# Three experts in plain fp32, two products side by side in the array, woven buffer by buffer with the five others

## The chip, the core and the metric

The kernel runs on one core of a Trainium2 chip. The time is device microseconds for one execution of the whole program. The kernel before takes 2594.24 us (median of 3 runs, 2590.64 to 2599.49).

## What is computed

Two decoder blocks of two layers each, one after the other, on 256 tokens of width 1024, in fp32. The change touches only the last part, the mixture of experts (MoE) that ends the second block: eight experts of hidden width 3584, and each token goes to two of them.

```python
def moe_swiglu(h, router, w_gate, w_up, w_down):
    bsz, seq, d = h.shape
    t = h.reshape(-1, d)
    logits = (t @ router).astype(jnp.float32)
    top_v, top_i = lax.top_k(logits, TOP_K)
    top_w = jax.nn.softmax(top_v, axis=-1)
    gates = jnp.sum(jax.nn.one_hot(top_i, N_EXPERTS, dtype=jnp.float32) * top_w[..., None], axis=1)
    out = jnp.zeros(t.shape, jnp.float32)
    for e in range(N_EXPERTS):
        y_e = swiglu(t, w_gate[e], w_up[e], w_down[e]).astype(jnp.float32)
        out = out + gates[:, e:e + 1] * y_e
    return out.astype(h.dtype).reshape(bsz, seq, d)
```

`swiglu(h, ...)` is `(silu(h @ w_gate) * (h @ w_up)) @ w_down`. The weights of the eight experts are 352 MB, of the 560 MB that the kernel reads.

## The kernel before

Products keep fp32 accuracy by splitting. Each operand x becomes H, x rounded to the format fp32r that TensorE takes in one pass, and L = x - H, also fp32r; `mm3` (line 226) then adds three products, H*H, H*L and L*H. `weights` (line 207) does this for weights: SyncE (SP) issues a load of 128 x 2048 numbers (1 MB) into a buffer of the ring `raw`, ScalarE (ACT) casts it into a buffer of the ring `wh` (line 222), VectorE (DVE) subtracts into one of the ring `wl` (line 223). The rings are lists of pools that are taken in turn; in the MoE there are 5 buffers of raw and 3 each of wh and wl. A raw buffer is free when the subtraction is done, wh and wl when TensorE (PE) is done with them.

The MoE begins by ranking the experts by how many tokens they got (`moe_order`, line 2068). The five fullest have 128 places (here: wide), the other three 64 (tight; `PLACES`, line 1980). `moe_gather` (line 2170) brings the tokens of a group of experts (`TOGETHER`, line 1982) into place with a one-hot product and splits them; `moe_places` makes the transposed one-hot for the way back. `moe_pass` (line 2241) then goes through the experts in order. An expert is four steps of 1024, 1024, 1024 and 512 hidden columns. For each step `half` does the gate product (four buffers of weights, two in the last step) and then the up product (as many); `gate` applies silu and `hidden` multiplies; `turn` transposes the result on PE and splits it; `down` multiplies by w_down (four buffers, two in the last step), adding up over the expert in two PSUM banks, `py`. That is 42 buffers an expert. In the program's order the gate and up products of step i+1 stand before the down product of step i. After an expert's last step `combine` splits the result, brings it back to the tokens with the transposed one-hot (lines 2347 and 2348), and adds it into the output, weighted by the gate (line 2349).

A tight expert uses the 64 free places otherwise: H and L of its tokens stand side by side in the 128 stationary columns, so two products a piece are enough (line 2263), with wh and with wl. They leave two partial results in partitions 0 to 63 and 64 to 127, which `whole` (line 2281) adds up.

PSUM has eight banks: four in pool "a" (`half`) and four in pool "b" (`turn`, `py`, `combine`, `moe_gather`, `moe_places`). A planner puts the instructions of each engine in order, by their place in the program and by when it reckons their inputs and buffers to be ready; on the chip each engine goes through its own list in that order. Line 751, in an earlier part of the kernel, is a plain fp32 product with 64 stationary columns; two heads in turn write to partitions 0 to 63 and 64 to 127 of the same bank, with line 752 behind each. After the MoE a branch handles tokens beyond an expert's places; here it isn't taken.

Of the kernel before, what the change touches and what calls it, by code (L numbers as in the profile page):

```python
# [11 lines left out]
F32 = mybir.dt.float32  # L12
# [42 lines left out]
class Core:  # L55
# [65 lines left out]
    @contextmanager  # L121
    def phase(s, raw, split, work):

        with ExitStack() as c:
            pool = lambda nm, n: c.enter_context(s.tc.tile_pool(name=f"{nm}{s.uid()}", bufs=n, reuse_waits="tile"))
            s.ring = {nm: [pool(nm, n)] * n for nm, n in (("raw", raw), ("wh", split), ("wl", split))}
            s.t2p = pool("t2", work)
            yield

    @contextmanager  # L130
    def wider(s, **more):

        with ExitStack() as c:
# [3 lines left out]
            s.turn = 0  # L137
            yield

    turn = 0  # L140
# [66 lines left out]
    def weights(s, src, k0, nk, c0, cn, rows="k p"):  # L207
# [5 lines left out]
        raw, H, L = (s.ring[nm][s.turn % len(s.ring[nm])].tile([128, 2048], dt, tag=nm, name=f"{nm}{s.n}")  # L213
                     for nm, dt in (("raw", F32), ("wh", F32R), ("wl", F32R)))
        s.turn += 1
# [8 lines left out]
        return v(H), v(L)  # L224

# [1750 lines left out]
class MoE:  # L1976
# [125 lines left out]
    def moe(s, N):  # L2102
# [6 lines left out]
        s.moe_pass(N, N.slot, s.PLACES, s.TOGETHER, first, ahead)  # L2109
# [3 lines left out]
        with s.tc.If(n > 0):  # L2113
            rest = s.small([128, 2, s.E], "slotb")
            nc.vector.tensor_sub(rest, N.slot, bc(s.caps, 2))
            s.moe_pass(N, rest, s.REST, s.TOGETHER_REST, s.moe_gather(N, rest, s.TOGETHER_REST[0], s.REST))
            s.moe_store()
# [52 lines left out]
    def moe_gather(s, N, slot, js, places):  # L2170
# [20 lines left out]
        for d in range(0, ND, 2):  # L2191
            p = s.psum("b")
            for m in range(2):
                for h, src in enumerate((N.H, N.L)):
                    for t in range(2):
                        nc.tensor.matmul(p[:, m * W:m * W + W], src[d // 2][:, t, m * 128:m * 128 + 128], P[:, t, :W],
                                         start=(h == 0 and t == 0 and m == 0), stop=(h == 1 and t == 1),
                                         skip_group_check=True)
            for m in range(2):
                x = s.t2([128, 512], "xe", F32R)  # L2200
                x = x[:, :2 * W].rearrange("p (a j c) -> p j a c" if wide else "p (j a c) -> p j a c", a=2, j=len(js))
                v, g = p[:, m * W:m * W + W].rearrange("p (j c) -> p j c", j=len(js)), s.col("ln_ffn_2", 8 + d + m)
                nc.scalar.activation(x[:, :, 0], v, AF.Copy, scale=g)
                nc.vector.scalar_tensor_tensor(x[:, :, 1], v, g, f(x[:, :, 0]), op0=OP.mult, op1=OP.subtract)
                X.append(x)
        return {j: [X, i, places[j], P] for i, j in enumerate(js)}

    def moe_places(s, N, G):
# [3 lines left out]
        p = s.psum("b")  # L2212
        n = next(iter(G.values()))[2]
        for X, i, n, P in G.values():
            for t in range(2):
                nc.tensor.matmul(p[:n, i:i + 1], f(P[:, t, i * n:i * n + n]), N.rc[:, t:t + 1], start=(i == 0 and t == 0),
                                 stop=(t == 1), skip_group_check=True)
        nc.vector.tensor_copy(rc[:n], p[:n, :len(G)])
        for g in G.values():
            X, i, n, P = g  # L2220
            PT = s.t2([128, 2, 128], "onehotT", F32R)
            x = P[:, :, i * n:i * n + n]
            if n == 64:
                y = s.t2([128, 512], "eyH", F32R)[:, :256].rearrange("p (t c) -> p t c", t=2)
                for u in range(2):
                    nc.vector.tensor_copy(y[:, :, u * 64:u * 64 + 64], f(x))
                x = y
            p = s.psum("b", dt=F32R)
            for t in range(2):
                nc.tensor.transpose(p[:, t * 128:t * 128 + 128], x[:, t], s.identR)  # L2230
            nc.scalar.copy(PT, p[:, :256].rearrange("p (t c) -> p t c", t=2))
            g += [PT, rc[:n, i:i + 1]]

    AHEAD = 3
    WIDE = 1024

# [4 lines left out]
    def moe_pass(s, N, slot, places, together, G, ahead=()):  # L2241
# [3 lines left out]
        steps = [(j, f0, min(s.WIDE, s.FE - f0)) for j in range(s.E) for f0 in range(0, s.FE, s.WIDE)]  # L2245
        per = len(steps) // s.E
        py = {}
        ahead = list(ahead)
        most = places is s.PLACES
# [7 lines left out]
        def product(o, j, x, w, start, stop):  # L2257


            if x.shape[2] == 64:  # L2260
                x = x.rearrange("p a c -> p (a c)")
                for h in range(2):
                    nc.tensor.matmul(o, x, w[h], start=start and h == 0, stop=stop and h == 1, skip_group_check=True)  # L2263
            else:
                s.mm3(o, (x[:, 0], x[:, 1]), w, start, stop)

        def half(i, nm):

            j, f0, fn = steps[i]
            X, u = G[j][:2]  # L2270
            p = [s.psum("a") for _ in range(fn // 512)]
            nk = 2048 // fn
            for k0 in range(0, ND, nk):
                w = ahead.pop(0) if ahead else weights(nm, j, 128 * k0, nk, f0, fn)
                for k in range(nk):
                    for c, o in enumerate(p):
                        product(o, j, X[k0 + k][:, u], [x[:, k, c * 512:c * 512 + 512] for x in w],
                                k0 + k == 0, k0 + k == ND - 1)
            return p

        def whole(p, n):

            if n == 128:
                return p
            a = s.t2([64, 512], "eb")
            nc.scalar.copy(a, p[64:])
            nc.vector.tensor_add(a, p[:64], a)
            return a

        def gate(i, pg):  # L2290
            n, rc = G[steps[i][0]][2], G[steps[i][0]][5]
            out = []
            for p in pg:
                out.append(s.t2([n, 512], "eh"))
                nc.scalar.activation(out[-1], whole(p, n), AF.Silu, scale=rc)
# [133 lines left out]
```

## Time and profile before

| | |
|---|---|
| median of 3 runs | 2594.24 us |
| the profiled execution | 2596.73 us, span 2595.0 us |
| granted TensorE clock, mean | 0.968 |
| PE busy over the span | 2423.1 us |
| VectorE busy | 2004.4 us |
| ScalarE busy | 1550.8 us |
| loaded from memory | 555.88 MB |

All rows come from one profiled execution; times in them are microseconds from its span's start unless marked ns. Busy time of an engine is the time in which it executes an instruction; matmuls overlap each other, so their pitch, the time from the start of one to the start of the next, tells more than their length. A wait is put down to the instruction that released it last.

### The profile page before, as it was taken

The numbers are of one execution on the slowest core, as the hardware profiler recorded it, in microseconds if no ns is written. First come the engines' busy times: TensorE is split into PE (matmuls) and PEld (weight loads), VectorE is DVE, ScalarE is ACT, GpSimd is POOL, SyncE is SP. The second block draws the span as 40 slices with busy tenths as digits, with TensorE's granted clock in tenths as the row PEclk, the third lists the DMA queues.
The fourth block names the chain that finished last, engine by engine and source line by source line (L and its number), as shares of the span: only waits on it lengthen the run. The fifth ranks groups of instructions, "written<-read, shape, count | busy, mean of one in ns | idle before, by whom it ended". The sixth has DMA issues, their size and how long they took to land.

```text
span 2595.0 us, 39887 instructions
## 1 busy us (share of the span) xinstructions
PE 2423.1 (93%) x15462; PEld 2122.8 (82%) x15462; DVE 2004.4 (77%) x3186; ACT 1550.8 (60%) x2313; POOL 88.0 (3%) x180
## 2 busy tenths in 40 slices
PE   7988799999998999899999999999999999988887
PEld 6867689999888999789999888888888877655654
DVE  6876477658886765766658876888888888999998
ACT  4553355445555544564455645776777777878776
POOL 2011010000001000000000000000000000000000
PEclk9998699999999999989999998999999999999999
DMA  5312345555434555425554213999999998999997
GB/s 166 111 58 34 62 166 167 178 178 162 131 109 137 165 178 183 146 82 184 183 172 130 87 45 131 343 359 349 368 329 365 346 360 325 371 379 363 372 369 281
DMA packets 266195, 559.59 MB, mean 216 GB/s; under 512 B 12751, under 2 KB 172510, under 8 KB 251662
## 3 DMA queue, kind: packets, MB, share of 16 engines
q1 hardware_dynamic: 264544, 555.71, 61.2%
q0 software_dynamic: 1328, 1.22, 0.9%
q8 instruction: 123, 2.02, 0.3%
q14 instruction: 74, 0.61, 0.1%
q10 hardware_dynamic: 126, 0.03, 0.0%
HBM read 555.88 MB, written 1.05 MB: 215 GB/s over the span
## 4 chain that ended last, share of the span: by engine, by line
PE 69%; DVE 15%; issue 6%; ACT 4%; POOL 2%; DMA 2%; DVEq 0%; ACTq 0%; POOLq 0%; SPq 0%
PE pa L230 16%; PE pa L231 16%; PE pa L229 16%; DVE wl L223 9%; ACT wh L222 2%; PE pb L230 2%; PE pb L231 2%; PE pb L229 2%; PE pb L1167 2%; PE pb L1792 2%; PE pa L2263 1%; PE pb L1481 1%; PE pb L2263 1%; PE pb L1133 1%; DMA ssmvb<-in_ssm_a_log_dram 1%
## 5 line engine op out<-in xcount | busy, mean ns | idle before, releaser
L223 DVE TENSOR_TENSOR wl<-raw,wh 128x512 fp32r<-128x512 f32 (+1 forms) x1108 | 1258.7, 1166 | 212.3 <-ACT wh L222 207.1
L222 ACT CAST wh<-raw 128x512 fp32r<-128x512 f32 (+1 forms) x1108 | 1063.6, 1004 | 559.3 <-issue 266.3
L229 PE MATMUL pa<-xH,wh 128*128 128x256 f32 (+1 forms) x1936 | 553.2, 286 | 16.0 <-ACT xH L313 8.1
L230 PE MATMUL pa<-xL,wh 128*128 128x256 f32 (+1 forms) x1936 | 553.3, 286 | 0.5 <-DVE xL L314 0.5
L231 PE MATMUL pa<-xH,wl 128*128 128x256 f32 (+1 forms) x1936 | 552.8, 286 | 1.0 <-DVE wl L223 1.0
L229 PEld LDWEIGHTS pa<-xH,wh 128*128 128x128 f32 (+1 forms) x1936 | 372.3, 193 | 18.1 <-ACT xH L313 8.8
L230 PEld LDWEIGHTS pa<-xL,wh 128*128 128x128 f32 (+1 forms) x1936 | 372.3, 192 | 3.5 <-DVE xL L314 2.0
L231 PEld LDWEIGHTS pa<-xH,wl 128*128 128x128 f32 (+1 forms) x1936 | 372.2, 192 | 2.9 <-DVE wl L223 1.9
L230 PE MATMUL pa<-wl,xe 128*128 128x512 f32 x560 | 221.1, 395 | 7.7 <-DVE wl L223 7.7
L231 PE MATMUL pa<-wh,xe 128*128 128x512 f32 x560 | 219.7, 392 | 0.0
L229 PE MATMUL pa<-wh,xe 128*128 128x512 f32 x560 | 207.7, 393 | 0.0
L2263 PE MATMUL pa<-wl,xe 128*128 128x512 f32 x336 | 131.2, 424 | 36.8 <-DVE wl L223 34.0
L229 PE MATMUL pa<-hidH,wh 128*128 128x256 f32 x528 | 149.4, 283 | 0.0
L230 PE MATMUL pa<-hidL,wh 128*128 128x256 f32 x528 | 149.4, 283 | 0.0
L231 PE MATMUL pa<-hidH,wl 128*128 128x256 f32 x528 | 149.4, 283 | 0.0
L230 PEld LDWEIGHTS pa<-wl,xe 128*128 128x128 f32 x560 | 105.7, 189 | 34.0 <-DVE wl L223 12.8
L2263 PE MATMUL pa<-wh,xe 128*128 128x512 f32 x336 | 123.7, 402 | 3.5 <-ACT wh L222 3.5
L229 PEld LDWEIGHTS pa<-wh,xe 128*128 128x128 f32 x560 | 105.6, 189 | 21.3
L231 PEld LDWEIGHTS pa<-wh,xe 128*128 128x128 f32 x560 | 105.6, 189 | 21.0
L2263 PEld LDWEIGHTS pa<-wl,xe 128*128 128x128 f32 x336 | 59.6, 192 | 76.3 <-DVE wl L223 67.0
L230 PE MATMUL pb<-wl,ehH 128*128 128x512 f32 x280 | 111.2, 397 | 0.9 <-DVE wl L223 0.9
L231 PE MATMUL pb<-wh,ehL 128*128 128x512 f32 x280 | 109.4, 391 | 0.0
(813 smaller groups left out, 4078.8 us busy)
## 6 DMA issues: line engine op xcount, KB each, us to landing
raw<-in_o_moe_w_gate_dram SPq DMA_DIRECT2D x112, 1024.0 KB
raw<-in_o_moe_w_up_dram SPq DMA_DIRECT2D x112, 1024.0 KB
raw<-in_o_moe_w_down_dram SPq DMA_DIRECT2D x112, 1024.0 KB
raw<-in_ffn_w_dram SPq DMA_DIRECT2D x60, 1024.0 KB
raw<-in_od_w_in_dram SPq DMA_DIRECT2D x20, 1024.0 KB
raw<-in_o_w_in_dram SPq DMA_DIRECT2D x16, 1024.0 KB
raw<-in_e_ffn_w_gate_dram SPq DMA_DIRECT2D x11, 1024.0 KB
raw<-in_e_ffn_w_up_dram SPq DMA_DIRECT2D x11, 1024.0 KB
```

Of the source, the lines that this page charges most:

```text
L222: nc.scalar.copy(H[:, c:e], raw[:, c:e])
L223: nc.vector.tensor_sub(L[:, c:e], raw[:, c:e], f(H[:, c:e]))
L229: mm(out, a[0], b[0], start=start, stop=False, skip_group_check=True)
L230: mm(out, a[0], b[1], start=False, stop=False, skip_group_check=True)
L231: mm(out, a[1], b[0], start=False, stop=stop, skip_group_check=True)
L1133: nc.tensor.matmul(p[:, k * 128:k * 128 + 128], NT[:, k, :], X[:, k, :], start=True, stop=True)
L1167: mm = lambda o, a, b, st=True, sp=True: nc.tensor.matmul(o, a, b, start=st, stop=sp, skip_group_check=True)
L1481: mm = lambda o, a, b, st, sp: nc.tensor.matmul(o, a, b, start=st, stop=sp, skip_group_check=True)
L1792: mm = lambda o, a, b, st=True, sp=True: nc.tensor.matmul(o, a, b, start=st, stop=sp, skip_group_check=True)
L2263: nc.tensor.matmul(o, x, w[h], start=start and h == 0, stop=stop and h == 1, skip_group_check=True)
```

## The change

The tight experts' weights are no longer split. They are loaded into a raw buffer (`whole_weights`) and multiplied as they are, in plain fp32, by 64 stationary columns of tokens that aren't split either. Each pair of products, for the two halves of the columns, writes to partitions 0 to 63 and 64 to 127 of one bank, so that they can stand side by side in the array. Their hidden values lie on 128 partitions with half as many columns, are transposed as 128 x 128 blocks and not split; their result is in one bank rather than two, and goes back to the tokens in plain fp32 with 64 rows.

The three tight experts also no longer come after the five wide ones. `moe_pass` is now two lanes (`moe_lane`), generators that yield after each buffer of weights: the wide lane starts with eight buffers (`LEAD`), then one buffer of the tight lane is put behind each 1.6 buffers of the wide one, so that both end together. All of the tight lane's PSUM banks but its result come from pool "a" (`side`); the wide lane keeps to its pools. The rings now have a turn of their own each, as raw is used without wh and wl. The tight gather stands behind the first eight buffers.

```diff
+    def buffer(s, nm):
+        i = s.turns[nm]
+        s.turns[nm] += 1
+        return s.ring[nm][i % len(s.ring[nm])].tile([128, 2048], F32 if nm == "raw" else F32R, tag=nm,
+                                                    name=f"{nm}{s.n}")
...
+    def whole_weights(s, src, k0, nk, c0, cn, rows="k p"):
+        s.n += 1
+        v = s.buffer("raw")[:, :nk * cn].rearrange("p (k c) -> p k c", k=nk)
+        s.nc.sync.dma_start(v, src[k0:k0 + 128 * nk, c0:c0 + cn].rearrange(f"({rows}) c -> p k c", p=128))
+        return v
...
+    LEAD = 8
...
-    def moe_pass(s, N, slot, places, together, G, ahead=()):
+    def moe_pass(s, N, first, ahead):
+        wide = [x for x in s.TOGETHER if s.PLACES[x[0]] == 128]
+        tight = [x for x in s.TOGETHER if s.PLACES[x[0]] == 64]
+        a = s.moe_lane(N, N.slot, s.PLACES, wide, first, ahead, True)
+        per = 3 * D * s.FE // (128 * 2048)
+        na, nb = per * sum(map(len, wide)), per * sum(map(len, tight))
+        for _ in range(s.LEAD):
+            next(a)
+        na -= s.LEAD
+        b = s.moe_lane(N, N.slot, s.PLACES, tight, s.moe_gather(N, N.slot, tight[0], s.PLACES, "a"), side="a")
+        due = 0
+        for _ in range(na):
+            next(a, None)
+            due += nb
+            while due >= na:
+                due -= na
+                next(b, None)
+        for x in (a, b):
+            for _ in x:
+                pass
...
-            return s.weights(w[e] if isinstance(e, int) else w[bass.ds(e, 1)].rearrange("o r c -> (o r) c"), *a)
+            w = w[e] if isinstance(e, int) else w[bass.ds(e, 1)].rearrange("o r c -> (o r) c")
+            return s.weights(w, *a) if places[j] == 128 else s.whole_weights(w, *a)
...
         def half(i, nm):
...
-            p = [s.psum("a") for _ in range(fn // 512)]
+            p = [s.psum("a") for _ in range(fn // 512 if wide else 1)]
             nk = 2048 // fn
+            hw = fn // 2
             for k0 in range(0, ND, nk):
                 w = ahead.pop(0) if ahead else weights(nm, j, 128 * k0, nk, f0, fn)
                 for k in range(nk):
...
+                    if wide:
+                        x = X[k0 + k][:, u]
+                        for c, o in enumerate(p):
+                            s.mm3(o, (x[:, 0], x[:, 1]), [x[:, k, c * 512:c * 512 + 512] for x in w], start, stop)
+                    else:
+                        for c in range(2):
+                            mm(p[0][64 * c:64 * c + 64, :hw], X[k0 + k][:, u], w[:, k, c * hw:c * hw + hw],
+                               start=start, stop=stop, skip_group_check=True)
+                yield
...
         def turn(i, h):
...
-                p = s.psum("b")
+                p = s.psum(side)
...
+                if wide:
+                    H, L = s.t2([128, n, 128], "ehH", F32R), s.t2([128, n, 128], "ehL", F32R)
+                    s.split(v, H, L)
+                    out.append((H, L))
                 else:
+                    y = s.t2([128, n, 128], "ehT")
+                    nc.scalar.copy(y, v)
+                    out.append(y)
...
         def down(i, hs):
...
-                py[j] = [s.psum("b"), s.psum("b")]
+                py[j] = [s.psum("b") for _ in range(2 if wide else 1)]
...
+                    else:
+                        a, q = divmod(k0 + k, fn // 256)
+                        for c in range(2):
+                            mm(py[j][0][64 * c:64 * c + 64], hs[0][:, q, 64 * a:64 * a + 64],
+                               w[:, k, c * 512:c * 512 + 512], start=start, stop=stop, skip_group_check=True)
+                yield
...
         def combine(j):
...
+                    p = s.psum(side)
+                    if wide:
+                        mm(p, PT[:, t, :], yH, start=True, stop=False)
+                        mm(p, PT[:, t, :], yL, start=False, stop=True)
+                    else:
+                        mm(p, f(PT[64 * c:64 * c + 64, t, :]), y[64 * c:64 * c + 64], start=True, stop=True)
```

## Rows read from the trace of the kernel before

**Rows 1.** The page, engines: busy us, share of the span, instructions.
```profile
PE 2423.1 (93%) x15462; PEld 2122.8 (82%) x15462; DVE 2004.4 (77%) x3186; ACT 1550.8 (60%) x2313; POOL 88.0 (3%) x180
```
**Rows 2.** Stretch: its us, busy PE PEld DVE ACT POOL, clock, DMA share, GB/s.
```profile
1620.00:2215.00 595.00, 585.47 (x2687) 481.83 (x2686) 518.50 (x329) 427.57 (x304) 0.00 (x0) 1.00 0.95 351
2240.00:2570.00 330.00, 276.58 (x1045) 190.34 (x1046) 314.92 (x217) 258.54 (x203) 0.00 (x0) 0.96 0.98 373
```
**Rows 3.** Timeline: start, length, what; first wide and tight products, combines.
```profile
1601.63 0.77 PE L229 MATMUL pa<-wh,xe 128*128 128x512 f32 x1
...
2225.76 0.39 PE L2263 MATMUL pa<-wh,xe 128*128 128x512 f32 x1
...
2253.64 0.63 PE L2347 MATMUL pb<-eyH,onehotT 128*128 128x512 f32 x2
...
2490.48 0.62 PE L2347 MATMUL pb<-eyH,onehotT 128*128 128x512 f32 x2
...
2584.14 0.74 PE L2347 MATMUL pb<-eyH,onehotT 128*128 128x512 f32 x2 [0.21 <-ACT eyH L288]
```
**Rows 4.** Timeline of PE: two fp32r products of 512 columns in a wide expert.
```profile
1700.02 0.39 PE L230 MATMUL pa<-wl,xe 128*128 128x512 f32 x1
1700.24 0.39 PE L231 MATMUL pa<-wh,xe 128*128 128x512 f32 x1
```
**Rows 5.** Groups from 1560 us on: count | busy us, mean ns | idle before.
```profile
L223 DVE TENSOR_TENSOR wl<-raw,wh 128x2048 fp32r<-128x2048 f32 x333 | 752.4, 2286 | 74.0 <-ACT wh L222 72.1
L222 ACT CAST wh<-raw 128x2048 fp32r<-128x2048 f32 x333 | 631.9, 1911 | 127.3 <-PE pa L231 62.2 <-PE pb L231 34.7 <-PE pb L2263 8.8
...
L291 DVE TENSOR_TENSOR ehL<-pb,ehH 128x512 fp32r<-128x512 f32 x35 | 24.0, 685 | 3.3 <-ACT ehH L288 3.3
L2295 ACT ACTIVATE eh<-pa,slotrc 128x512 f32<-128x512 f32 x35 | 23.1, 687 | 19.5 <-PE pa L231 19.5
L2349 DVE SCALAR_TENSOR_TENSOR hT<-pb,gates,hT 128x512 f32<-128x512 f32 x32 | 22.4, 743 | 2.2 <-PE pb L2348 2.2
...
L288 ACT CAST ehH<-pb 128x512 fp32r<-128x512 f32 x35 | 20.5, 585 | 32.8 <-PE pb L2311 32.8
```
**Rows 6.** Waits (us in total, times, longest): 1660 to 2210, then 2240 to 2560.
```profile
PEld pa L230 <- DVE wl L223: 12.8, 14, 1.5
...
PEld pa L2263 <- DVE wl L223: 62.4, 68, 2.5
```
**Rows 7.** Line 751 alone: records, ns min/median/max, first and last start.
```profile
L751 PEld LDWEIGHTS pb<-mt,xd x64: 132/134/137, 647.4 to 770.0; 128*64 128x64 f32 x64
L751 PE MATMUL pb<-mt,xd x64: 379/390/431, 647.4 to 770.2; 128*64 128x256 f32 x64
```
**Rows 8.** Timeline of PE: plain fp32 products across the full array, and the next.
```profile
352.12 1.11 PE L561 MATMUL pb<-kmem,xq 128*128 128x256 f32 x4
352.88 0.59 PE L229 MATMUL pa<-wh,xH 128*128 128x512 f32 x1
```
**Rows 9.** Timeline of PE around the plain fp32 products of 64 columns.
```profile
647.05 0.28 PE L229 MATMUL pa<-xH,wh 128*128 128x256 f32 x1
647.17 0.28 PE L230 MATMUL pa<-xL,wh 128*128 128x256 f32 x1
647.38 0.66 PE L751 MATMUL pb<-mt,xd 128*64 128x256 f32 x4
647.86 0.40 PE L752 MATMUL pb<-mt,xd 128*64 128x128 f32 x4
648.19 0.49 PE L737 MATMUL pb<-cumR,twice 64*128 64x512 f32 x1
```
**Rows 10.** SP's waits from 1600 us on: us in total, times, longest.
```profile
SPq L217 <- DVE wl L223: 720.1, 304, 7.2
```
**Rows 11.** Busy time by stretch, as in rows 2: two of 20 us.
```profile
2420.00:2440.00 20.00, 17.18 (x66) 12.25 (x65) 19.71 (x14) 16.76 (x13) 0.00 (x0) 0.91 1.02 392
2460.00:2480.00 20.00, 16.96 (x64) 11.31 (x64) 18.81 (x11) 16.16 (x12) 0.00 (x0) 1.00 1.02 397
```

More of the change, by code (lines that the diff above doesn't have):

```diff
@@ L2108, in moe @@
         s.moe_order(N)
-        s.moe_pass(N, N.slot, s.PLACES, s.TOGETHER, first, ahead)
+        s.moe_pass(N, first, ahead)
         s.moe_store()
@@ L2206, in moe_gather, with moe_places @@
         return {j: [X, i, places[j], P] for i, j in enumerate(js)}
-    def moe_places(s, N, G):
+    def moe_places(s, N, G, side="b"):
         nc = s.nc
         rc = s.small([128, len(G)], "slotrc")
-        p = s.psum("b")
-        n = next(iter(G.values()))[2]
+        p = s.psum(side)
+        Y = []
         for X, i, n, P in G.values():
[L2215 to L2222, printed above, removed]
+            y = P[:, :, i * n:i * n + n]
@@ L2243, in moe_pass, with moe_lane @@
+    def moe_lane(s, N, slot, places, together, G, ahead=(), most=False, side="b"):
         nc = s.nc
         I = s.i
-        steps = [(j, f0, min(s.WIDE, s.FE - f0)) for j in range(s.E) for f0 in range(0, s.FE, s.WIDE)]
-        per = len(steps) // s.E
+        G = dict(G)
+        mm = nc.tensor.matmul
+        js = [j for x in together for j in x]
+        steps = [(j, f0, min(s.WIDE, s.FE - f0)) for j in js for f0 in range(0, s.FE, s.WIDE)]
+        per = len(steps) // len(js)
         py = {}
@@ L2275, in half @@
                 for k in range(nk):
[L2276 to L2288, printed above, removed]
+                    start, stop = k0 + k == 0, k0 + k == ND - 1
@@ L2352, in moe_pass @@
         n = len(steps)
-        pg = half(0, "gate")
+        pg = yield from half(0, "gate")
         if most:
             s.moe_rms(N)
-        s.moe_places(N, G)
+        s.moe_places(N, G, side)
         h = gate(0, pg)
-        h = hidden(0, h, half(0, "up"))
+        h = inner(0, h, (yield from half(0, "up")))
         for i in range(n):
             j, f0, fn = steps[i]
-            if f0 == s.WIDE and j + 1 < s.E and j + 1 not in G:
-                g = s.moe_gather(N, slot, next(x for x in together if j + 1 in x), places)
-                s.moe_places(N, g)
+            if f0 == s.WIDE and i + per < n and steps[i + per][0] not in G:
+                g = s.moe_gather(N, slot, next(x for x in together if steps[i + per][0] in x), places, side)
+                s.moe_places(N, g, side)
                 G |= g
-            pg = half(i + 1, "gate") if i + 1 < n else None
+            pg = (yield from half(i + 1, "gate")) if i + 1 < n else None
             hs = turn(i, h)
@@ L2368, in moe_pass @@
                 h = gate(i + 1, pg)
-                h = hidden(i + 1, h, half(i + 1, "up"))
-            down(i, hs)
+                h = inner(i + 1, h, (yield from half(i + 1, "up")))
+            yield from down(i, hs)
             if f0 + fn == s.FE:
```

119 lines of the change are left out of this document (60 added, 59 removed).

## Prediction

> **What bounds the kernel now.** I read the page's engine rows first, then the busy time by stage, then single groups, pitches and waits inside each stage. Over the whole span TensorE is busy 93% and VectorE 77% [rows 1], an average that hides two stages. While the five wide experts run (1620 to 2215 us), PE is busy 585.5 of 595 us and VectorE 518.5; while the three tight ones run (2240 to 2570 us), VectorE is busy 314.9 of 330 us and PE only 276.6, at a granted clock of 0.96 [rows 2]. So the first stage is PE's and the second VectorE's, and each leaves the other engine unused. The transfers are not idle in either: 351 and 373 GB/s [rows 2].
>
> Three readings carry the sum. First, the calendar. The first wide product starts at 1601.63, the first tight one at 2225.76; the last combine of a wide expert begins at 2253.64, that of the second tight expert at 2490.48, of the third at 2584.14, and the span ends at 2595.0 [rows 3]. A tight expert therefore takes (2490.48 - 2253.64)/2 = 118.4 us, or 2.82 us for each of its 42 buffers. Between 2225.76 and 2253.64 PE does the last two wide "down" buffers (24 products) and, for the rest, tight work. Second, the price of a product: one fp32r product of 512 columns follows the other after 0.22 to 0.23 us [rows 4]; I use 0.227, the mean over longer runs of them. A wide buffer is 12 of them, 2.72 us; a tight one is 8, 1.82 us. Third, the splitting: every buffer costs ACT 1.911 us and VectorE 2.286 us [rows 5]. 2.286 plus the smaller VectorE work is the 2.82 us of a tight buffer; that PE waits there for VectorE's wl is in the waits: 62.4 us on one line against 12.8 us in the wide stage [rows 6].
>
> **The change part by part.**
>
> *Splitting removed.* 126 of 336 buffers are no longer split: 126 x 2.286 = 288 us less for VectorE and 126 x 1.911 = 241 us less for ACT. Gone too is the addition of halves at line 2287. VectorE would then have some 210 x 2.286 = 480 us of splitting plus about 150 us of small work to do in roughly 890 us, so it is no longer the bound. Late next is PE, which now has to carry the whole MoE.
>
> *Plain fp32 products, side by side.* An fp32 product shows as two records: line 751 runs 32 times and has 64 records [rows 7]. Across the full array four records of 256 columns take from 352.12 to 352.88 [rows 8], nearly 0.21 us each with the first one's start-up; that is twice the columns' time of fp32r. Do two 64-column products overlap? Line 751 and 752 answer it: two heads, written to partitions 0 to 63 and 64 to 127 of one bank, are 4 records of 256 and 4 of 128 columns. One after the other they would take 4 x 0.215 + 4 x 0.107 = 1.29 us; the next product starts 0.81 us after the first [rows 9]. In pairs they need 0.64, so 0.17 us is start-up, and 0.09 us more passes on the way in (0.21 us after the product before, whose own pitch is 0.12) [rows 9]. The loads of 64 columns, 134 ns each [rows 7], hide under a record. For 512 columns a record is 2 x 0.2135 = 0.427 us, and a tight buffer has two k-rows of two records each, side by side: 4 x 0.427 = 1.71 us, plus 0.26 us for entering and leaving = 1.97 us; 126 of them, 248 us. The entry is paid once a buffer because buffers of the two kinds alternate.
>
> *Small tight work.* Transposes: 14 an expert on 128 partitions, 42 x 0.12 = 5 us. Combining: four plain fp32 products of 512 columns an expert, 12 x 0.854 = 10 us. Sum 15 us. The tight gather keeps its size; it only comes earlier. The silu and the gating product act on 128 x half as many columns, off PE's path.
>
> *Wide work.* Unchanged in number. From 1601.63 to 2253.64 are 652 us, of which 27.9 - 24 x 0.227 = 22.4 us were tight work: 630 us, with gathers, transposes, combines and the waits of that stage. Some of these waits were for VectorE (12.8 us [rows 6]) and may shrink: down to -13 us.
>
> *The weave.* After eight wide buffers one tight buffer follows each 1.6 wide ones in the priority order, and the planner puts PE's and SP's queues in that order. The tight stage as a stage disappears: PE's sum is 630 + 248 + 15 = 893 us from 1601.63, so about 2494.6. The end behind the last combine stays 2595.0 - 2584.14 = 10.9 us: the store waits for the same four additions; the wide lane's own last combine comes just ahead. That gives 2505.5 us if PE never waits for anything new.
>
> *Waits added.* (a) A tight matmul now waits on a landing itself, and its raw buffer is released by PE instead of VectorE. Queued behind it on PE are the wide products; on SP the next load waits for that buffer (SP waited 720.1 us for VectorE's release in this part [rows 10], so this release is what paces loading). With five raw buffers, a load issued when tight buffer k is done has the time of the next four buffers, about 3 x 3.0 + 1.97 = 11 us, to land and be split; split is 1.911 + 2.286 = 4.2 us, which leaves nearly 7 us for the landing of 1 MB that at 373 GB/s takes 2.8 us. I take it as covered; if two loads collide it costs up to 2.8 us at a time. (b) PSUM banks. Tight holds one of the four "a" banks during its gate and up halves and one of the four "b" banks throughout. At each of 20 gate-to-up changes a wide half finds one bank free and needs a second; its predecessor's first bank was complete 0.68 us (three products) before the end and its silu takes 0.69 us [rows 5], so it is nothing with ACT free and about 0.5 us if ACT is in a cast. In 15 steps the second transposed block waits for the first one's cast and subtraction, 0.585 + 0.685 us [rows 5], or more behind a split; part of it under other products: about 1 us. 20 x 0.5 + 15 x 1.0 = 25 us is my estimate; bounds 0 (a tight buffer of 1.97 us stands in between) and, with each wait also behind a full cast and a full subtraction, 20 x 2.6 + 15 x 5.5 = 135 us. I take it near the low end because both engines have lost a third of their load.
>
> Forecast: 2505.5 + 25 = 2530.5 for the span. The profiled execution took 2596.73 for its 2595.0, and the median is 2.5 below that, so 0.8 comes off: **2530 us**.
>
> **The rivals.**
>
> *Transfers take over.* 328 buffers of 1.0486 MB remain after the eight that are loaded early, 344 MB from about 1611 us on. My forecast asks for about 375 GB/s on average. For a limit: the tight stage held 373 GB/s over 330 us. Against: VectorE was saturated there, and single 20 us stretches reached 392 and 397 GB/s [rows 11]. If 373 were the limit: 344/0.373 = 922, end of loading 2533, plus landing, one tight buffer, combine and store, about 17 us: 2550. If the wide stage's 351 were it: 980 us, and 2608: no gain at all.
>
> The Trainium skill, "DMA: Bandwidth & Descriptors", Specifications and "Where 436 GB/s comes from", puts the HBM limit of a core at about 358 GB/s and says that it binds loads into SBUF. By that rule loading would take some 961 us and the end would stay near 2590; the rows of the tight stage, 373 GB/s over 330 us, already exceed it, so I give the case of no gain little.
>
> *Banks (the slower side).* The mechanism is (b) above: PE is the bound and stands still in order whenever its next product lacks a bank, with tight's long-lived accumulators holding two of eight. The gain before waits is 2595 - 2505.5 = 90 us over 35 places; from 2.6 us a place on it is a loss. At the upper bound, 135 us plus the wide combines' 5 x 4 x 0.74 = 15 us (an addition each [rows 5]), it ends at 2655. For it: PE runs in order and the casts are long. Against: ACT and VectorE are at 70% at most, and the planner can place other ready products there.
>
> *The pairs don't overlap.* Then the change does not do what it says: 126 x 1.71 = 215 us more, about 2745. The spacing in [rows 9] speaks against it.
>
> *Better than the sum.* No new waits and 13 us fewer old ones: 2492, if the landing keeps up at close to 390 GB/s.
>
> **How the numbers follow.** Forecast (2505 to 2555) 0.60; transfers at about 373 GB/s (2545 to 2578) 0.15; no gain by 351 to 358 GB/s or milder banks (2587 to 2602) 0.05; banks to a loss 0.09; no overlap 0.03; better than the sum 0.08. The range 2497 to 2578 leaves out the slower cases and half of the last. What a measurement can tell from no change here is 0.3%, about 8 us. Faster 0.60 + 0.15 + 0.08 + 0.01 of the case of no gain = 0.84; same, its other 0.04; slower 0.09 + 0.03 = 0.12.
>
> **What the profile of the changed kernel would show.** Right: no stage with VectorE above 90%; PE above 93% from 1610 to the end at clock 1.0; tight fp32 records in pairs some 10 ns apart with 0.43 us to the next pair and 1.9 to 2.0 us a buffer; big subtractions down to about 210; loading at 370 to 380 GB/s evenly; wide experts stretched to about 178 us. Wrong: tight records 0.43 us apart singly (no overlap); PE idle before L2311's transposes or the first product of a half with ACT or VectorE as releaser, tens of us in all (banks); PE waiting on raw landings with DMA share at 1.0 (transfers).

## The result, and the profile after

The changed kernel takes 2692.26 us, median of four executions, of which three lie between 2690.6 and 2692.8; the kernel before, on the same chip, 2596.39, median of four. The ratio is 1.037, 95% interval 1.0344 to 1.0395: 3.7% slower, where 2530 and a gain of 2.5% were forecast. (The fourth, at a granted clock of 0.926 instead of 0.973, is left out of the ratio.) The profiled execution took 2692.8 us for a span of 2691.0.

In the changed kernel the wide products stand on lines 240 to 242, the cast and the subtraction on 226 and 227, the tight gate and up products on 2321, the tight down products on 2378; SP loads split buffers on line 221 and whole ones on 234. First the page's engine row, as in [rows 1], then the two stretches of [rows 2]:

```profile
PE 2543.5 (95%) x15516; PEld 1997.9 (74%) x15516; DVE 1683.4 (63%) x2974; ACT 1282.8 (48%) x2124; POOL 88.0 (3%) x180
```
```profile
1620.00:2215.00 595.00, 570.98 (x2223) 327.56 (x2221) 309.70 (x207) 257.35 (x203) 0.00 (x0) 0.99 0.88 322
2240.00:2570.00 330.00, 316.55 (x1191) 174.62 (x1190) 171.18 (x106) 138.95 (x99) 0.00 (x0) 1.00 0.90 330
```

What was meant to happen to VectorE happened: it fell from 2004 to 1683 us and is now 52% busy in both stretches. PE is busy 96% in both, at a granted clock of 0.99 and 1.00, and loading has fallen to 322 and 330 GB/s. So PE is the bound, as forecast, but it is busy for 120 us more than before. That is the question: what does PE do in a time in which it is busy and no faster?

The tight products' groups in the whole trace (count | busy us, mean ns | idle before) answer where:

```profile
L2321 PE MATMUL pa<-raw,xf 128*64 128x512 f32 (+1 forms) x768 | 231.7, 555 | 0.2 <-ACT ehT L2358 0.2
L2378 PE MATMUL pb<-raw,ehT 128*64 128x512 f32 x336 | 126.3, 611 | 0.0
```

358 us, with no idle time ahead of them, where the prediction has 126 buffers at 1.97 us, 248. The timeline of PE shows how (start, length, what; records that follow one another on one line are joined):

```profile
2003.15 0.39 PE L242 MATMUL pb<-wh,ehL 128*128 128x512 f32 x1
2003.47 1.07 PE L2321 MATMUL pa<-raw,xf 128*64 128x512 f32 x2
2004.47 0.73 PE L240 MATMUL pa<-wh,xe 128*128 128x512 f32 x2
...
2007.34 0.61 PE L240 MATMUL pa<-wh,xe 128*128 128x512 f32 x2
2007.88 1.07 PE L2321 MATMUL pa<-raw,xf 128*64 128x512 f32 x2
2008.88 0.50 PE L241 MATMUL pa<-wl,xe 128*128 128x512 f32 x1
```

A tight product is two records. Here a single product, one column half of the array, stands between wide ones, twice within 5 us: 1.00 us from its start to the next wide product, for a quarter of a buffer, while the other half of the array has nothing. At 2007.88 it stands behind two wh products (x2 on line 240) and ahead of the wl product of line 241. PE's list, which is made before anything runs, has such places throughout. One of them, with what each product waits for ("x3" is three in a row; the trace has this sequence from 2379.88 us on, and again from 2464.61):

```
12504 L2321 MATMUL pa2618_21988<-raw2637_22121,xf2117_18193 64x512 x3
12505 L240 MATMUL pa2631_22059<-wh2638_22128,xe2471_20837 128x512 [waits Activation_49]
12506 L240 MATMUL pa2632_22060<-wh2638_22128,xe2471_20837 128x512
12507 L2378 MATMUL pb2456_20753<-raw2639_22146,ehT2616_21984 64x512 [waits DMAHW2_49]
12508 L2378 MATMUL pb2456_20753<-raw2639_22146,ehT2616_21984 64x512 x2
12509 L241 MATMUL pa2631_22059<-wl2638_22129,xe2471_20837 128x512 [waits DVE_49]
...
12519 L2378 MATMUL pb2456_20753<-raw2639_22146,ehT2616_21984 64x512
```

Of one tight buffer (raw2639) three products stand in the gap between ACT's cast and VectorE's subtraction of a wide buffer, and the fourth behind that wide buffer. In the next buffer it is one and three. I counted the stays of PE on 64-column products in the trace (a stay lasts from the first start to the start of the next other product): 240, where the prediction has 126. 102 of them are two records, one product alone (median 1.003 us); 107 are six records, of which four run side by side and two alone (1.861 us). Only 672 of the 1104 records start beside another one.

The end is as forecast: the last wide combine starts at 2678.32, the last tight one at 2680.36, 10.6 us before the end of the span.

```profile
2678.32 0.50 PE L2395 MATMUL pb<-eyH,onehotT 128*128 128x512 f32 x1
...
2680.36 1.99 PE L2398 MATMUL pa<-ey,onehotT 64*128 64x512 f32 x8
```

The waits of the stretch from 1610 to 2680 us (in total, times, longest) show nobody who holds PE up for long; SP now waits for PE:

```profile
DVE wl L227 <- ACT wh L226: 250.4, 111, 8.0
ACT wh L226 <- DMA raw<-in_o_moe_w_down_dram: 107.9, 37, 6.0
...
PE pa L241 <- DVE wl L227: 24.0, 23, 2.6
PE pb L241 <- DVE wl L227: 10.8, 13, 2.4
PE pa L240 <- ACT wh L226: 3.5, 5, 1.3
PE pb L240 <- ACT wh L226: 0.4, 2, 0.2
PE pb L2349 <- DVE ehL L302: 0.2, 1, 0.2
...
SPq L234 <- PE pa L2321: 346.0, 66, 8.2
SPq L234 <- PE pb L2378: 178.7, 31, 7.4
SPq L221 <- DVE wl L227: 178.5, 79, 5.1
```

### The profile page after: what moved, and what is told of

It is laid out like the page before. It is cut to its first block, busy times and chain, and to the rows that moved or that the text cites. A ratio compares the mean times of both kernels' runs of the same rounds, so it can differ in the third digit from the quotient of the medians.

```text
span 2691.0 us, 39312 instructions
## 1 busy us (share of the span) xinstructions
PE 2543.5 (95%) x15516; PEld 1997.9 (74%) x15516; DVE 1683.4 (63%) x2974; ACT 1282.8 (48%) x2124; POOL 88.0 (3%) x180
## 4 chain that ended last, share of the span: by engine, by line
PE 76%; DVE 10%; issue 4%; ACT 4%; POOL 2%; DMA 2%; SPq 0%; DVEq 0%; ACTq 0%; POOLq 0%
PE pa L241 16%; PE pa L240 15%; PE pa L242 15%; PE pa L2321 7%; DVE wl L227 5%; PE pb L2378 4%; PE pb L241 2%; ACT wh L226 2%; PE pb L242 2%; PE pb L240 2%; PE pb L1178 2%; PE pb L1803 1%; PE pb L1492 1%; PE pb L1144 1%; DMA raw<-in_o_moe_w_up_dram 1%
## 5 line engine op out<-in xcount | busy, mean ns | idle before, releaser
L227 DVE TENSOR_TENSOR wl<-raw,wh 128x512 fp32r<-128x512 f32 (+1 forms) x982 | 975.1, 1021 | 398.5 <-ACT wh L226 387.3
L226 ACT CAST wh<-raw 128x512 fp32r<-128x512 f32 (+1 forms) x982 | 823.0, 887 | 703.9 <-issue 265.0
L241 PE MATMUL pa<-wl,xe 128*128 128x512 f32 x560 | 231.3, 413 | 24.1 <-DVE wl L227 24.0
L2321 PE MATMUL pa<-raw,xf 128*64 128x512 f32 (+1 forms) x768 | 231.7, 555 | 0.2 <-ACT ehT L2358 0.2
L242 PE MATMUL pa<-wh,xe 128*128 128x512 f32 x560 | 221.4, 395 | 0.0
L240 PE MATMUL pa<-wh,xe 128*128 128x512 f32 x560 | 212.8, 410 | 3.6 <-ACT wh L226 3.5
L241 PEld LDWEIGHTS pa<-wl,xe 128*128 128x128 f32 x560 | 106.3, 190 | 102.4 <-DVE wl L227 44.3
L2321 PEld LDWEIGHTS pa<-raw,xf 128*64 128x64 f32 x768 | 58.9, 135 | 100.2 <-issue 92.3
L2378 PE MATMUL pb<-raw,ehT 128*64 128x512 f32 x336 | 126.3, 611 | 0.0
L2337 DVE SCALAR_TENSOR_TENSOR eh<-pa,slotrc,eh 128x512 f32<-128x512 f32 (+1 forms) x47 | 33.4, 733 | 131.4 <-PE pa L242 68.2
```

Source lines behind the costliest of these rows:

```text
L226: nc.scalar.copy(H[:, c:e], raw[:, c:e])
L227: nc.vector.tensor_sub(L[:, c:e], raw[:, c:e], f(H[:, c:e]))
L240: mm(out, a[0], b[0], start=start, stop=False, skip_group_check=True)
L241: mm(out, a[0], b[1], start=False, stop=False, skip_group_check=True)
L242: mm(out, a[1], b[0], start=False, stop=stop, skip_group_check=True)
L2321: mm(p[0][64 * c:64 * c + 64, :hw], X[k0 + k][:, u], w[:, k, c * hw:c * hw + hw], start=start, stop=stop, skip_group_check=True)
```

## The experiments

Two theories of the loss. A: the order breaks up the buffers, and each break costs PE time. The rival: the weave itself, or the fp32 form, costs that much, whatever the order (transfers, banks, no overlap). Eleven kernels were run; ratios are against the kernel before on the same chip, with 95% intervals.

**The products of a buffer together** (e1_together). Only the priority of the tight products changes; a ready buffer's four products then follow one another in PE's list.

```diff
+    FIRST = 1000
...
-                        for c in range(2):
-                            mm(p[0][64 * c:64 * c + 64, :hw], X[k0 + k][:, u], w[:, k, c * hw:c * hw + hw],
-                               start=start, stop=stop, skip_group_check=True)
+                        with s.rank(-s.FIRST):
+                            for c in range(2):
+                                mm(p[0][64 * c:64 * c + 64, :hw], X[k0 + k][:, u], w[:, k, c * hw:c * hw + hw],
+                                   start=start, stop=stop, skip_group_check=True)
```

The products of down get the same line.

> The changed kernel with one thing added: the planner gets the plain fp32 products of a tight buffer 1000 places earlier in priority, so that the four products of a buffer stand together in PE's list. In the changed kernel the list puts one of the four alone between the two wh products and the wl products of a wide buffer and the other three behind that wide buffer. Theory A (the loss is broken pairs and twice as many entries into the 64-column form): the visits fall from 240 to about 126, a tight buffer on PE from about 3.0 us to 1.96 us, and some 130 us go: 2692 - 130, about 2560 us. Theory B (a shortage of raw buffers or of transfers, since ACT waits 252 us for landings in the changed kernel): the visits fall, but PE then waits for landings and the time stays above 2640 us. Theory C (too few PSUM banks): PE waits for evacuations, time above 2620 us, DMA share below 0.9.

Measured: 2566.23 us, ratio 0.9888 (0.9864 to 0.9911): 126 us less than the changed kernel, and 1.1% faster than the kernel before. All 1104 records now run in pairs, in 122 stays; they take 248.2 us, and the prediction's price of a buffer comes out at 1.868 us a stay plus 0.09 us on the way in (0.318 us behind the last wide product instead of 0.227), 1.96 for 1.97. (What the price lacks is the first wide product behind a stay: the next one starts 0.34 us after it, from 2005.69 to 2006.03 below, instead of 0.23.) The timeline of PE and the tight groups of this kernel:

```profile
2003.51 0.39 PE L242 MATMUL pb<-wh,ehL 128*128 128x512 f32 x1
2003.83 1.94 PE L2323 MATMUL pa<-raw,xf 128*64 128x512 f32 x8
2005.69 0.50 PE L240 MATMUL pb<-wh,ehH 128*128 128x512 f32 x1
2006.03 0.40 PE L241 MATMUL pb<-wl,ehH 128*128 128x512 f32 x1
```
```profile
L2323 PE MATMUL pa<-raw,xf 128*64 128x512 f32 (+1 forms) x768 | 165.8, 559 | 5.6 <-DMA raw<-in_o_moe_w_gate_dram 5.3 <-ACT ehT L2360 0.2
L2381 PE MATMUL pb<-raw,ehT 128*64 128x512 f32 x336 | 82.3, 610 | 0.0
```

The whole buffer takes 1.86 us in one stay (2003.83 to 2005.69); in the changed kernel it took 1.003 + 1.861 in two. The time PE spends from start to start on tight records falls from 356.7 to 248.2 us (108.5), that on the wide products, where the ways into and out of the stays are counted, from 660.7 to 644.3 (16.4). Together that is 125 of the 126 us. SP's loads stand in the same order in both kernels but for 4 of 336 places. Theory A holds, with its size.

**Only two thirds of them together** (e5_gateup): the same, without the lines around down.

> The tight products of gate and up are put ahead as in the kernel with all of them together (2566 us), those of down are left to the planner as in the kernel after (2692 us). Theory A (each broken visit costs PE time): in the trace of after the 42 buffers of down took 124.9 us in 85 visits, together they would take 42 x 1.87 = 78.5 us, so about 46 us of loss come back, with 43 more entries at 0.09 us 50: about 2614 us. Rival (what helped was that tight products ran early and gave up their raw buffers early, whatever their pairs): a third of the tight buffers released later again should cost a third of 126 us at most, 42, and if the gate and up part is what matters for loading, nearly nothing: 2566 to 2585 us, and the visits of down would not be longer.

Measured: 2602.21 us, ratio 1.004 (1.0023 to 1.0057): 36 us above the kernel with all of them together (39 by the ratios), below the 46 to 50 of theory A and above the rival's 0 to 19, though within the 42 that the rival names as its most. So the time doesn't decide, with SP's loads in the same order in both kernels. What decides is whether the products of down took longer, as only theory A has it: the tight groups of this kernel,

```profile
L2323 PE MATMUL pa<-raw,xf 128*64 128x512 f32 (+1 forms) x768 | 164.6, 556 | 6.5 <-DMA raw<-in_o_moe_w_gate_dram 6.3 <-ACT ehT L2360 0.2
L2380 PE MATMUL pb<-raw,ehT 128*64 128x512 f32 x336 | 126.1, 611 | 0.0
```

with gate and up at the price of e1_together and down at that of the changed kernel, in 84 stays, 42 of them one product alone. The products of down cost 44 us more, of which 36 show in the time: the rest may have been hidden in waits for loads (below); that isn't shown.

**Four products in another order** (e3_inturn): in e1_together, both products of one column half first, then both of the other.

```diff
-                for k in range(nk):
-                    for c in range(2):
+                for c in range(2):
+                    for k in range(nk):
```

> As e1_together, but the four products of a tight buffer stand in another order: both of the first half of the columns, then both of the second half. So the two middle ones are the only neighbours that write to different halves of the partitions. If only neighbours in the list stand side by side, a visit takes 3 x 0.854 + 0.26 = 2.8 us in place of 1.96, and the time is about 107 us above e1_together. If each half of the columns goes through its own products whatever the order, a visit takes 1.96 us and the time is that of e1_together. If nothing overlaps, 3.7 us and 220 us above.

Measured: 2563.89 us in one execution. A stay of four products takes 1.874 us, against 1.868. So the two halves overlap although only the two middle products are neighbours of different halves in the list; with four products it was enough that both halves had work in it. It has a limit: a buffer of the narrow last step has eight products of 256 columns, and with four of one half ahead of four of the other 12 of its stays took 2.79 us, against 1.878 in e1_together.

**The tight experts behind the wide ones** (e2_behind): the changed kernel without the loop that weaves.

> The changed kernel without the weave: the tight lane's buffers come behind all of the wide lane's; everything else as changed (plain fp32, pairs, banks, tight gather behind the first eight buffers). Here no wide product stands between tight ones, and neither VectorE (no splitting), nor PE (1.71 us a buffer and no entries) can be the bound in the tight stage: it shows how fast the 126 MB can come. Theory A: pairs whole, so about 2230 us for the wide part and then 126 buffers at the transfers' pace, 2.5 to 2.8 us each (415 to 373 GB/s): 2555 to 2595 us. Theory B (the transfers cannot do better than in the tight stage before, 373 GB/s): 2590 to 2600 us, no change against before. If the pairs did not overlap even when adjacent, a tight buffer would take 3.4 us of PE: 2665 us.

Measured: 2556.96 us, ratio 0.9866 (0.9842 to 0.989). The stretch of the wide experts and 200 us of the tight ones (columns as in [rows 2]):

```profile
1620.00:2215.00 595.00, 587.30 (x2687) 484.63 (x2687) 519.46 (x316) 429.16 (x304) 0.00 (x0) 1.00 0.96 352
2320.00:2520.00 200.00, 158.76 (x706) 47.95 (x704) 10.63 (x15) 9.45 (x16) 0.00 (x0) 1.00 1.02 411
```

The first is close to that of the kernel before (PE 585.47, 351 GB/s). In the second VectorE is 5% busy, PE 79%, and the loads run at 411 GB/s at a DMA share of 1.02, a buffer every 2.55 us: this is the transfers' own pace here, not the 373 GB/s of [rows 2], where VectorE held them. So plain fp32 in pairs brings its gain without any weave, and the weave, kept in order, brings no more: it has used PE's slack (PE is 96% busy in the stretch of e1_together shown below), but something else is now short.

The rest of the runs asks what that is: e1_together stands 36 us above the forecast. The wide products take 644 us from start to start in it, 589 in e2_behind (584.1 for the 2500 of 2520 that the trace holds). PE's waits in e1_together from 1610 to 2540 us:

```profile
PE pb L241 <- DVE wl L227: 17.0, 13, 2.6
PE pa L241 <- DVE wl L227: 7.9, 8, 1.6
PE pa L2323 <- DMA raw<-in_o_moe_w_gate_dram: 5.3, 2, 4.2
PE pb L2209 <- DVE xe L2220: 1.0, 1, 1.0
PE pb L2351 <- DVE eh L2339: 0.9, 3, 0.4
```

**Less work for VectorE** (e8_quarter): in e1_together, VectorE subtracts a quarter of each wide buffer.

```diff
+                if q == 2048:
+                    e = 512
                 nc.vector.tensor_sub(L[:, c:e], raw[:, c:e], f(H[:, c:e]))
-        return v(H), v(L)
+        return v(H), L[:, :512].rearrange("p (k c) -> p k c", k=1) if q == 2048 else v(L)
```

> All tight products together; of each wide buffer VectorE subtracts only the first 512 of 2048 columns and every wl product reads these (the other wl are left out, so what is computed is a part of the reference). PE has the same products. Theory B (what is left over the forecast, 2566 against 2530, is PE waiting for VectorE's wl, and raw buffers that VectorE gives back late): VectorE's work on a buffer falls from 2.29 to about 0.6 us, the 25 us of waits on wl go, and the time falls to 2530 to 2542 us. Rival C (the loads cannot keep up with the demand, about 370 GB/s): the waits turn up again as waits on ACT's wh, which waits for landings, and the time stays at 2555 to 2566 us.

Measured: 2561.49 us, ratio 0.9885 (0.9843 to 0.9927), no different from e1_together. VectorE is 25% busy, the wide products take 646 us, about as in e1_together, and the waits have moved to ACT's casts:

```profile
1620.00:2215.00 595.00, 576.29 (x2556) 363.70 (x2555) 149.80 (x235) 289.89 (x227) 0.00 (x0) 1.00 0.96 369
```
```profile
PE pa L249 <- ACT wh L226: 14.9, 16, 1.9
PE pb L250 <- DVE wl L229: 4.4, 6, 1.0
PE pa L2332 <- DMA raw<-in_o_moe_w_gate_dram: 4.2, 2, 3.1
ACT wh L226 <- DMA raw<-in_o_moe_w_gate_dram: 79.0, 31, 5.4
ACT wh L226 <- DMA raw<-in_o_moe_w_down_dram: 75.8, 34, 4.7
```

The waits on wl were late casts handed on, and the casts wait for landings (the last two lines). Theory B is out.

**Pieces of half a buffer** (e6_halves): `s.piece = 1024` in place of 2048 in e1_together.

> All tight products together; each wide buffer is cast and subtracted in two pieces of 1024 columns (one row of weights each) instead of one of 2048. From landing to the last subtraction it takes about 0.96 + 2 x 1.2 = 3.3 us instead of 4.2, and the first four of twelve products can start earlier. Theory B (latency of the split holds PE and raw buffers): waits on wl fall by half or more and the time is 2535 to 2555 us. Rival C (loads): 2562 to 2570 us. Rival D (more and smaller instructions cost ACT and VectorE more than the latency gives): 2570 us or more.

Measured: 2575.65 us, ratio 0.9926 (0.9897 to 0.9956): rival D, 9 us worse by the medians, though the intervals just overlap. The shorter way through the split buys nothing, which fits a shortage ahead of it.

**Half of each tight load** (e9_halfload): in e1_together, the second half of each tight buffer's rows is left out, and its products read the first half again.

```diff
-        s.nc.sync.dma_start(v, src[k0:k0 + 128 * nk, c0:c0 + cn].rearrange(f"({rows}) c -> p k c", p=128))
-        return v
+        n = nk // 2
+        s.nc.sync.dma_start(v[:, :n], src[k0:k0 + 128 * n, c0:c0 + cn].rearrange(f"({rows}) c -> p k c", p=128))
+        return v[:, :n]
...
-                               X[k0 + k][:, u], w[:, k, c * hw:c * hw + hw],
+                               X[k0 + k][:, u], w[:, k // 2, c * hw:c * hw + hw],
```

> All tight products together as in the 2566 us kernel; of each tight buffer only the first half of the rows is loaded (0.52 instead of 1.05 MB) and the products of the second half read it again, so part of the reference's weights is left out. PE has the same products in the same places, ACT and VectorE the same work; what has to be loaded falls from 344 to 278 MB. In the 2566 us kernel the wide products take 644 us from start to start, in the kernel with the tight experts behind 588. Theory C (the loading, at a DMA share of 0.92 to 1.01 through five buffers handed on in turn, is what holds the woven kernel above the forecast): the waits of the wide products, some 35 to 45 us, go, and the time falls to 2515 to 2540 us. Theory B (VectorE's and ACT's splitting and the order on PE hold it): the time stays at 2555 to 2568 us.

Measured: 2515.82 us, ratio 0.9697 (0.9677 to 0.9717): 50 us less, at the lower end of theory C. The wide stretch of e1_together, and then of this kernel, with this one's largest waits of PE:

```profile
1620.00:2215.00 595.00, 571.24 (x2527) 364.00 (x2526) 349.43 (x232) 289.69 (x225) 0.00 (x0) 0.99 0.96 368
```
```profile
1620.00:2215.00 595.00, 585.89 (x2650) 379.50 (x2649) 367.88 (x244) 302.92 (x234) 0.00 (x0) 1.00 0.85 313
```
```profile
PE pa L242 <- DVE wl L227: 3.7, 6, 1.0
PE pa L2324 <- DMA raw<-in_o_moe_w_gate_dram: 2.9, 2, 2.8
PE pb L242 <- DVE wl L227: 1.5, 2, 1.0
```

DMA share 0.85 instead of 0.96, PE 98.5% busy instead of 96.0, waits on wl 5 us instead of 25; the wide products fall from 644 to 614 us (scaled to 2520), the tight ones from 248 to 236. From the first wide product to the last combine PE now needs some 903 us, where the prediction's sum without the banks has 893; 0.11 us behind each of 113 stays, 12 us, is about the difference. So PE's part of the sum was right but for that, and the loading is what the woven kernel lacks.

**The depth of the ring** (e4_four, e11_wl2, e12_wh2): e1_together with four raw buffers instead of five (`s.wider(raw=1)` around the MoE left out), and with six, paid for with one of three wl or one of three wh.

> All tight products together; four raw buffers instead of five. The prediction held five to cover the loading with 7 us for a landing of 3 us. If the ring is deep enough, a buffer less leaves 4 us for it and the time moves by less than 10 us: 2564 to 2576. Theory B' (the ring that both kinds of buffers share in a fixed turn is what holds loading up, since a tight buffer waits for its turn behind VectorE): each buffer less makes loads start one buffer, about 2.7 us, later in a share of the 328 loads, and the time rises by 40 us or more: above 2605.

> All tight products together; six raw buffers instead of five and two wl buffers instead of three (the same memory). In the 2566 us kernel a raw buffer is held some 13.5 us from its issue to its release, by either kind, and five of them give a pace of 2.7 to 2.85 us; one less cost 42 us. Theory C (the ring, not PE or VectorE, sets the pace): a sixth buffer brings 10 to 30 us, 2535 to 2556 us, against what the lost wl buffer takes, and the wide products' 644 us fall towards the 625 they take with half of the tight loads. Rival (the transfers' own rate is the limit, so that more buffers only make each landing take longer): 2560 to 2570 us, with landings later by about one buffer's 2.7 us. If two wl buffers are too few, PE waits for wl grow and it is 2575 us or more.

> As the one with two wl buffers, but with three wl and two wh. wh is written first and read last by a wide buffer's products, so it is held longer than wl: PE would wait more. Theory C gives 2540 to 2560 us, and if wh is short 2570 us or more; if both kernels with six raw buffers stay at 2560 to 2570 us, the ring's depth no longer counts.

Measured: 2608.36 with four (ratio 1.0064, 1.0035 to 1.0092), 2557.77 with six and two wl (0.9887, 0.9855 to 0.9919), 2575.62 with six and two wh (0.9932, 0.9907 to 0.9957). One buffer less costs 42 us, as theory B' said; one more brings nothing that the intervals tell from e1_together. From the issue of a load to the release of its buffer pass 12.0 us for a wide buffer with four, 13.7 with five and 16.4 with six and two wl (means between 1650 and 2480 us). Of the last 2.7 us little is the landing (7.4 us after the issue with five, 8.0 with six), so it isn't what the rival expected either: the buffers lie longer with their data in them, a tight one 6.2 us before PE takes it, after 4.1 with five. Whether the missing wl ate the gain can't be told from these runs, in which the parts ahead of the MoE have the other rings too.

**Half of the tight work woven** (e10_halfweave): `due += nb // 2` in e1_together.

> All tight products together, but one tight buffer follows each 3.2 wide ones instead of 1.6, and the other half of the tight work comes behind the wide lane. Woven stage: 202 wide buffers at 2.72 us and 63 tight ones at 1.97 with the rest of the wide stage's work, about 745 to 760 us, asking for some 370 GB/s; behind it about 63 buffers at 2.55 us, the pace of the transfers when the tight experts run alone, 160 us. Theory C (the woven kernel is close to both PE's and the transfers' limit and pays for the collisions): fewer collisions in the woven part, 2530 to 2550 us. Against it (the loss is a fixed price a visit or a fixed loss of loading wherever kinds alternate): 2555 to 2570 us, as with all of it woven or none.

Measured: 2587.92 us, ratio 0.9974 (0.9959 to 0.9989), slower than either end of the scale, and outside both expectations. The wide products take 640 us (635.0 for 2501 of 2520) although half as many buffers stand between them. The wide stretch and PE's largest waits from 1610 to 2420 us:

```profile
1620.00:2215.00 595.00, 564.79 (x2507) 398.35 (x2506) 400.89 (x256) 331.00 (x250) 0.00 (x0) 0.99 0.93 349
```
```profile
PE pa L241 <- DVE wl L227: 19.3, 17, 1.8
PE pb L241 <- DVE wl L227: 14.4, 11, 1.6
```

So the loss of the weave isn't in proportion to the stays. It isn't simply a full DMA either: the share there is 0.93, at 349 GB/s. PE's waits on wl, 34 us against 25 in e1_together, are a part of it; what makes them stays open.

## Why the prediction was wrong

The step that failed is one sentence, with the half-sentence on the weave that it rests on: "The entry is paid once a buffer because buffers of the two kinds alternate", and "the planner puts PE's and SP's queues in that order". The program alternates by buffer; PE's list does not. The planner places each product by itself. A tight product needs no cast and no subtraction, only a landing, and wherever a wide buffer's wl products are not ready yet, one or three of the four are put in that place and the rest behind (102 lone products in 240 stays). That the planner does so because it reckons a gap there is my reading of the list; that the order costs the time is shown by e1_together, which changes only the priority of these products. I had costed the step from an earlier part of the kernel in which the products of both halves happen to stand together [rows 9], and didn't ask what keeps them together here.

- *The price of a buffer in pairs*, 1.97 us: right (1.96 in e1_together) once it is together, but for a term that the prediction doesn't have, the first wide product behind a stay. It is followed only after 0.34 us (medians 0.337 in the changed kernel, 0.341 in e1_together), where wide products with wide ones around them follow after 0.228: 0.11 us a stay, some 13 us over 122 stays and 26 over 240. [rows 9] ends before such a product. Broken, a buffer is 1.003 + 1.861 us and a second way in, 1.09 more, and 0.11 again on the second way out.
- *The rival that pairs don't overlap*: its sign came ("records 0.43 us apart singly"), for 432 of the 1104 records, and for a reason that I hadn't on the list. Its 2745 us is what a break in every pair would cost; the hardware overlaps as [rows 9] showed.
- *VectorE off the bound*: right, 52%.
- *Banks*, 25 us and the slower rival: wrong. PE waits for evacuations under 1 us in all in the changed kernel (line 2349 above) and some 3 us in e1_together. The slower side came by another way than the one that I had priced.
- *Waits added, (a)*, "covered": wrong for the woven kernel. The working leaves "nearly 7 us" for a landing and prices it at 2.8 us, the transfer alone. From issue to landing 6.6 us pass on average in the wide stage of the kernel before (1650 to 2200 us), and 7.4 in e1_together, so next to nothing of the 7 was spare. With the order mended, what is late next is loading: 2566 instead of 2530, and 2516 with half of the tight loads. This is the rival "transfers take over" (2550, 2545 to 2578), though not by its fixed limit: the same queues carry 411 GB/s in the tight stage of e2_behind, and through five buffers in a fixed turn about 368 in the weave, where a buffer fewer costs 42 us. By what exactly the weave loses that rate is open.
- The Trainium skill, "DMA: Bandwidth & Descriptors", "Where 436 GB/s comes from", by which about 358 GB/s bind loads into SBUF: the 411 GB/s over 200 us of e2_behind, on this one core, speak against it as a limit here.

The sum for the changed kernel, from what was measured: forecast 2530, less 25 of banks, plus 125 of broken buffers with their ways in and out, plus what the loads, the waits on wl and the way out cost e1_together above the rest (2566 - 2505 = 61): 2691 of 2692.

## What to carry to other kernels

A price for a group of instructions holds only as long as something keeps the group together. Ask of every group that is cheap because it is together (two halves of the array, one entry into another form) who sets the order of its members on the engine, and read the engine's list, not the program. A small ready instruction that is put into a gap of the list costs the entry into the other form, and here left half of the array empty. Before weaving two kinds of work, try them one behind the other, since here that (2557) was as good as the best weave (2558 to 2566) at less trouble.

## What the runs showed of the hardware

- Two column halves of the array ran side by side even with two products of the one ahead of two of the other in the list (1.874 against 1.868 us, in one execution of e3_inturn), but no longer fully with four ahead of four (2.79 against 1.878 us).
- Coming to 64-column products from full-width ones cost 0.09 us, whether one product followed or four (0.318 us instead of 0.227). It goes with the tile and not with the fp32 form alone: in the kernel before, the fp32 transposes of line 2311 start 0.239 us behind a wide product where they use the full array (128*128, median of 31), and 0.327 where they use 64 rows (64*128, median of 12). The way out is partly in the stay's length (1.003 us for the 2 x 0.427 of a lone product) and partly in the first wide product behind it (0.34 us instead of 0.23). The Trainium skill, "TensorEngine Tiling (Array Packing)", Key Properties, says that a change of tiling mode drains the engine. The trace agrees in so far as each way in costs 0.09 us, the median both of the 240 stays and of the 122; whether the engine drains, it doesn't show.
- Loads of 1 MB ran at 411 GB/s over 200 us on this one core. A packet of 8192 bytes took 315 ns on average then (2300 to 2520 us), and 350 in the wide stage of the same kernel (1650 to 2200), with a twentieth of them at 606 ns or more instead of 321. VectorE's work alone isn't the reason: in the kernel before they took 349 ns in the wide stage (1650 to 2200), where VectorE is 87% busy, and 333 in the tight one (2240 to 2570), where it is 95% busy. What is stays open.
